# A Strassen-type output product of a SwiGLU layer: the second round of products accumulated on sums of the first, weight sums formed in place, and the GpSimd additions between the rounds taken out

## The chip, the cores and the metric

The kernel runs on one core of a Trainium2 chip. The metric is the device time of one execution in microseconds. A run gives a time of its own; a profiled execution gives a span (first to last instruction) and, beside it, that execution's time. All times of instructions below are microseconds from the start of the span.

## The reference, cut to what matters

The program is one decoder layer (sequence of 512, model width 1024): a token-mixing part with three gated branches, then a feed-forward part. Only the last product of the feed-forward part is touched here.

```python
x = x + merged @ w_o[l]
hf = rms_norm(x, ffn_norm_g[l]) @ w_ffn_in[l]
gt, up = jnp.split(hf, 2, axis=-1)
x = x + (jax.nn.silu(gt) * up) @ w_ffn_out[l]      # (512 x 2816) @ (2816 x 1024)
return x
```

All inputs and outputs are fp32. The kernel does each fp32 product as three TensorE products of split operands: a high part (fp32r, a ScalarE cast into a `wh` tile) and a low part (a VectorE difference into a `wl` tile); the function `mm3` issues hi x hi, hi x lo and lo x hi.

## The kernel before

The 2816 hidden columns are taken in two chunks (lines 890 to 902): 12 blocks of 128 first, then 10. For each chunk `ffn_in` computes the gated hidden activations and `quarters` (line 761) writes the seven left operands of a Strassen-type scheme for each pair of blocks; then `ffn_out` (line 806) multiplies them by `w_ffn_out` and adds the result to the residual stream `x1`. With `n` pairs (6, then 5), the scheme cuts the weight of a pair into four 128x512 quarters b11, b12, b21, b22 and needs seven products 1 to 7. Each product has two row blocks of 128 (`i` = 0, 1), so it fills two PSUM banks of 128x512 and takes 2 x 3 = 6 matmuls a pair. PSUM has eight banks here: four with the tag `mm`, three with `z`, one with `o`.

Seven products of two banks would need 14 banks, so the work is done in two rounds. The first round (lines 827 to 842) runs products 1, 7 and 6 over all pairs. The second (lines 854 to 872) runs products 2, 3, 4 and 5 over all pairs, product 2 on the banks `p1` that product 1 has left there. Between the rounds (lines 845 to 852) ScalarE copies p1 to SBUF (s1), VectorE forms s2 = p6 + s1 and s3 = p7 + s2 (temporaries of tag `t`, six buffers), and GpSimd adds s2 and s3 to three of the four quadrants of `x1` (tile `v` in the profile). Then product 3 takes a `z` and the `o` bank, product 4 two `mm` banks, product 5 two `z` banks. In the last pair the second round's products run in reverse (5, 4, 3, 2), and line 876 adds the banks to `x1`. In the second chunk (`last`) the final additions go to `t` temporaries which ScalarE's queue writes to `out` (line 878).

A pair's weights come by one DMA on SyncE's queue into a `raw` tile (three buffers). Its operands are made by `wsplit`: a ScalarE cast (line 81) and a VectorE difference (line 82), into `wh` and `wl` tiles of three buffers each, two per pair: in the second round first the one for products 2 and 3 (b21, b22 as loaded), then the one for products 4 and 5 (weight sums t1 and t4, lines 861 to 865, made in a `tt` tile of two buffers, with one `t` temporary for a partial sum). A `wh` buffer comes free when the matmuls that read it are done.

TensorE's instructions stand in the order of the source; on the other engines a scheduler orders them by priority (`tc.high_priority` moves loads and weight sums ahead), and each engine runs its own list strictly in order.

Of the kernel before, what the change touches and what calls it, by code (L numbers as in the profile page):

```python
# [11 lines left out]
ALU = mybir.AluOpType  # L12
# [23 lines left out]
def hybrid_layer(ctx, tc, x, mix_norm_g, w_in, q_norm_g, k_norm_g, w_attn_out, conf_dw_w,  # L36
# [5 lines left out]
    nc = tc.nc  # L42
    x, w_in, w_o = x[0], w_in[0], w_o[0]
# [16 lines left out]
    def alloc(tag, shape=(P, S), dt=F32):  # L60
        count[0] += 1
        where = ps if tag in ("mm", "z", "o") else odd if tag in ("c", "cf") else sb
        return where.tile(list(shape), dt, tag=tag, name=f"{tag}_{count[0]}", bufs=BUFS[tag])

    def psum(tag="mm"):
        return alloc(tag)

    def tmp(dt=F32, shape=(P, S)):
        return alloc("t", shape, dt)
# [22 lines left out]
    def mm3(o, a, b, start, stop):  # L92
        mm(o, a[0], b[0], start, False)
        mm(o, a[0], b[1], False, False)
        mm(o, a[1], b[0], False, stop)
# [45 lines left out]
    def wsplit(src):  # L141
        nsplit[0] += 1
        kt, n = src.shape[1], src.shape[2]
        with tc.high_priority(), ExitStack() as behind:
            for ins in queued_after.get(nsplit[0], ()):
                behind.enter_context(tc.issue_after(ins))
            hi, lo = alloc("wh", (P, kt, n), F32R), alloc("wl", (P, kt, n), F32R)
            split_to(hi, lo, src, sub=nc.gpsimd.tensor_sub if nsplit[0] in POOLW else None)
        return hi, lo
# [125 lines left out]
    with tc.high_priority(offset=1000000):  # L275
        for t in range(NT):
# [10 lines left out]
            last = nc.scalar.activation(y, y, AF.Exp, scale=-0.5)  # L287
# [518 lines left out]
    def ffn_out(j0, h, last):  # L806
        n = len(h)
        rows_of = lambda j, k: w_ffn_out[(j0 + 2 * j + k) * P:(j0 + 2 * j + k + 1) * P]

        def products(j, p, w, banks, start, stop):  # L810
            for i in range(2):
                a = [t[:, i * P:(i + 1) * P] for t in h[j][p]]
                mm3(banks[i], a, w, start and j == 0, stop and j == n - 1)

        def parts(src):
            hi, lo = wsplit(src)
            return [(hi[:, i], lo[:, i]) for i in range(src.shape[1])]

        def sums(fn):
            with tc.high_priority():  # L820
                t = alloc("tt", (P, 2, S))
                fn(t[:, 0], t[:, 1])
            return t


        p1, p6, p7 = [[psum(tag) for _ in range(2)] for tag in ("mm", "mm", "z")]
        for j in range(n):
            with tc.high_priority():
                w = alloc("raw", (P, 3, S))
                nc.sync.dma_start(w[:, 0:2], rows_of(j, 0).rearrange("p (n f) -> p n f", n=2))  # L830
                nc.sync.dma_start(w[:, 2], rows_of(j, 1)[:, S:])
            b11, b12, b22 = [w[:, i] for i in range(3)]

            def t32(t3, t2):
                nc.vector.tensor_sub(t3, b22, b12)
                nc.vector.tensor_add(t2, t3, b11)

            one, = parts(w[:, 0:1])
            t3, t2 = parts(sums(t32))
            products(j, 1, one, p1, True, True)  # L840
            products(j, 7, t3, p7, True, True)
            products(j, 6, t2, p6, True, True)

        x = lambda i, c: x1[c][:, i, :]
        for i in range(2):
            s1, s2, s3 = tmp(), tmp(), tmp()
            nc.scalar.copy(s1, p1[i])
            nc.vector.tensor_add(s2, p6[i], s1)  # L848
            nc.vector.tensor_add(s3, p7[i], s2)
            nc.gpsimd.tensor_add(x(i, 1), x(i, 1), s2)  # L850
            nc.gpsimd.tensor_add(x(i + 2, 0), x(i + 2, 0), s3)
            nc.gpsimd.tensor_add(x(i + 2, 1), x(i + 2, 1), s3)
        p3, p4, p5 = [[psum(tag) for tag in tags] for tags in (("z", "o"), ("mm", "mm"), ("z", "z"))]
        for j in range(n):
            with tc.high_priority():
                w = alloc("raw", (P, 2, 2, S))
                nc.sync.dma_start(w, w_ffn_out[(j0 + 2 * j) * P:(j0 + 2 * j + 2) * P].rearrange(
                    "(k p) (n f) -> p k n f", p=P, n=2))
            (b11, b12), (b21, b22) = [[w[:, k, i] for i in range(2)] for k in range(2)]

            def t14(t1, t4):
                v = tmp()
                nc.vector.tensor_sub(t1, b12, b11)
                nc.vector.tensor_sub(v, b22, b21)  # L864
                nc.vector.tensor_sub(t4, v, t1)  # L865

            two, three = parts(w[:, 1])
            t1, t4 = parts(sums(t14))
            order = [(2, two, p1, False), (3, three, p3, True), (4, t4, p4, True),
                     (5, t1, p5, True)]  # L870
            for p, part, banks, start in order if j < n - 1 else order[::-1]:
                products(j, p, part, banks, start, True)

        def add(i, c, p, final, op=nc.vector.tensor_add):
            y = tmp() if last and final else x(i, c)
            op(y, x(i, c), p)  # L876
            if last and final:
                nc.scalar.dma_start(out[i * P:(i + 1) * P, c * S:(c + 1) * S], y)

        for i in range(2):  # L880
            add(i, 1, p5[i], False)
            add(i + 2, 1, p5[i], True)
        for i in range(2):
            add(i + 2, 0, p4[i], True, nc.vector.tensor_sub)
        for i in range(2):
            add(i, 1, p3[i], True)
        for i in range(2):
            add(i, 0, p1[i], True)

    j0 = 0  # L890
    for c, n in enumerate((12, 10)):
        h = []
        queue.extend(ffn_in(j0, n, h, {k: list(v) for k, v in SPACE.items()}))
        if c == 0:
            tick(4)
            for square in [turn(f) for f in range(4, KT)]:
                square()
            tick(1)
            second_norm()
        drain()  # L900
        ffn_out(j0, h, c == 1)
        j0 += n
# [31 lines left out]
```

## Time and profile before

| | |
|---|---|
| median of 3 runs | 858.46 us (857.78 to 859.46) |
| the profiled execution's own time | 858.28 us |
| its span | 856.2 us |
| TensorE (PE) busy | 826.7 us, 97% of the span |
| VectorE (DVE) busy | 612.6 us, 72% |
| ScalarE (ACT) busy | 393.0 us, 46% |
| GpSimd (POOL) busy | 53.5 us, 6% |
| mean granted TensorE clock | 0.986 |
| first change of rounds (6 pairs) | about 636 to 655 us |
| second change of rounds (5 pairs) | about 810 to 829 us |

A row of the timeline has the start, the length, the engine, the line, the operation, output<-inputs by tile tag, the shape, the count of instructions merged into the row, and in square brackets the idle time of the engine ahead of it with what ended it. A row of the chain has start, length, engine, output tag, line and count. The view of stretches gives busy time of each engine (and number of instructions) between two points, with the granted TensorE clock (PEclk, 1.00 is full).

### The profile page before, as it was taken

How to read it: one execution, taken by the hardware profiler on the slowest of the kernel's cores; microseconds unless marked ns; L12 is line 12 of the kernel's file. 1: busy time of each engine (PE TensorE's matmuls, PEld its weight loads, DVE VectorE, ACT ScalarE, POOL GpSimd, SP SyncE). 2: the span in 40 equal slices, each digit the busy share in tenths (PEclk: the TensorE clock that was granted, in tenths of full speed). 3: DMA queues.
4: the chain of work that ended last, by engine and by line, in shares of the span. 5: the costliest groups of instructions: out<-in, count | busy, mean ns of one | idle time of the engine just before them, and what ended most of it. 6: DMA issues, size and time to landing. Idle time of an engine off the chain costs nothing.

```text
span 856.2 us, 9698 instructions
## 1 busy us (share of the span) xinstructions
PE 826.7 (97%) x3727; PEld 685.4 (80%) x3727; DVE 612.6 (72%) x878; ACT 393.0 (46%) x577; POOL 53.5 (6%) x72
## 2 busy tenths in 40 slices
PE   6999999999999999999999999999996999999967
PEld 6888887888888888888888888888875788888846
DVE  6598699896999998865443565556689645566895
ACT  6346689876663222753333453333332323333521
POOL 3100011101000000000001200000012000000040
PEclk9999999999999999999999999999997999999979
DMA  7333023131113323222452133322354422323532
GB/s 247 103 98 124 25 68 129 50 99 50 50 50 106 107 84 129 80 87 98 151 194 99 50 98 99 99 96 77 111 185 147 148 99 98 99 87 111 184 99 98
DMA packets 71274, 90.11 MB, mean 105 GB/s; under 512 B 1920, under 2 KB 56380, under 8 KB 71228
## 3 DMA queue, kind: packets, MB, share of 16 engines
q1 hardware_dynamic: 70060, 87.39, 31.0%
q10 hardware_dynamic: 1168, 2.10, 0.6%
q8 instruction: 29, 0.48, 0.2%
q14 instruction: 17, 0.14, 0.1%
HBM read 87.39 MB, written 2.10 MB: 105 GB/s over the span
## 4 chain that ended last, share of the span: by engine, by line
PE 91%; DVE 6%; issue 1%; ACT 1%; DMA 1%; SPq 0%; DVEq 0%
PE mm L90 76%; PE z L90 11%; PE o L90 3%; DVE t L864 1%; DVE wl L82 1%; DVE tt L865 1%; DMA m<-in_x_dram 1%; DVE cf L502 0%; DVE t L876 0%; PE mm L705 0%; DVE t L848 0%; DVE v L876 0%; ACT wh L81 0%; DVE t L283 0%; DVE t L82 0%
## 5 line engine op out<-in xcount | busy, mean ns | idle before, releaser
L90 PE MATMUL mm<-u,wh 128*128 128x512 f32 x1536 | 474.8, 390 | 1.0 <-DVE v L876 1.0
L90 PEld LDWEIGHTS mm<-u,wh 128*128 128x128 f32 x1536 | 287.3, 188 | 60.6 <-issue 1.4
L90 PE MATMUL mm<-u,wl 128*128 128x512 f32 x768 | 299.2, 390 | 0.0
L81 ACT CAST wh<-raw 128x1024 fp32r<-128x1024 f32 (+1 forms) x154 | 147.0, 955 | 286.8 <-PE mm L90 230.8
L82 DVE TENSOR_TENSOR wl<-raw,wh 128x1024 fp32r<-128x1024 f32 (+1 forms) x152 | 168.6, 1109 | 66.3 <-ACT wh L81 65.8
L90 PEld LDWEIGHTS mm<-u,wl 128*128 128x128 f32 x768 | 144.2, 188 | 30.2
L502 DVE SCALAR_TENSOR_TENSOR cf<-cf,cols_w,cf 128x512 f32<-128x512 f32 x120 | 89.9, 750 | 3.7 <-ACT cf L500 1.2
L793 DVE TENSOR_TENSOR t<-mm,cf 128x512 f32<-128x512 f32 x22 | 15.2, 691 | 59.6 <-PE mm L90 59.6
L90 PE MATMUL mm<-wh,m 128*128 128x512 f32 x104 | 37.4, 412 | 13.5 <-ACT wh L81 13.5
L81 ACT CAST wh<-tt 128x1024 fp32r<-128x1024 f32 x22 | 23.1, 1052 | 44.4 <-DVE tt L865 20.9
L90 PE MATMUL mm<-m,wh 128*128 128x512 f32 x128 | 39.4, 389 | 0.0
L90 PEld LDWEIGHTS mm<-wh,m 128*128 128x128 f32 x104 | 20.9, 201 | 18.7 <-ACT wh L81 14.4
L82 DVE TENSOR_TENSOR wl<-tt,wh 128x1024 fp32r<-128x1024 f32 x22 | 26.9, 1222 | 10.0 <-ACT wh L81 9.9
L791 DVE TENSOR_TENSOR t<-mm,cf 128x512 f32<-128x512 f32 x22 | 15.1, 688 | 25.9 <-PE mm L90 25.8
L90 PE MATMUL z<-wh,m 128*128 128x512 f32 x84 | 31.5, 415 | 0.0
L90 PEld LDWEIGHTS mm<-m,wh 128*128 128x128 f32 x128 | 24.0, 188 | 4.9
L78 ACT ACTIVATE s<-s 128x384 f32<-128x384 f32 (+1 forms) x48 | 26.9, 561 | 1.2
L717 POOL TENSOR_TENSOR cf<-cf,t 128x512 f32<-128x512 f32 x7 | 9.9, 1417 | 255.3 <-ACT t L715 255.0
L850 POOL TENSOR_TENSOR v<-v,t 128x512 f32<-128x512 f32 x4 | 6.0, 1502 | 310.6 <-DVE t L848 310.6
L90 PE MATMUL mm<-m,wl 128*128 128x512 f32 x64 | 24.9, 389 | 0.0
L90 PE MATMUL mm<-wh,b 128*128 128x512 f32 x72 | 23.9, 389 | 0.0
L90 PE MATMUL mm<-wl,m 128*128 128x512 f32 x52 | 21.5, 414 | 1.8 <-DVE wl L82 1.8
(254 smaller groups left out, 1087.8 us busy)
## 6 DMA issues: line engine op xcount, KB each, us to landing
raw<-in_w_in_dram SPq DMA_DIRECT2D x23, 1024.0 KB
raw<-in_w_ffn_in_dram SPq DMA_DIRECT2D x22, 1024.0 KB
raw<-in_w_ffn_out_dram SPq DMA_DIRECT2D x11, 1024.0 KB
raw<-in_w_ffn_out_dram SPq DMA_DIRECT2D x11, 512.0 KB
raw<-in_w_in_dram SPq DMA_DIRECT2D x10, 512.0 KB
raw<-in_w_o_dram SPq DMA_DIRECT2D x4, 1024.0 KB
raw<-in_w_ffn_out_dram SPq DMA_DIRECT2D x11, 256.0 KB
m<-in_x_dram SPq DMA_DIRECT2D x8, 256.0 KB
```

The costliest lines, as they stand in the source:

```text
L78: table(nc.scalar.activation(o, i, f, **kw))
L81: (copy or nc.scalar.copy)(hi, src)
L82: (sub or nc.vector.tensor_sub)(lo, src, hi.bitcast(F32))
L90: nc.tensor.matmul(o, lhsT, rhs, start=start, stop=stop, skip_group_check=True)
L502: nc.vector.scalar_tensor_tensor(y, pad[:, n:n + S], w(n), y, ALU.mult, ALU.add)
L717: nc.gpsimd.tensor_add(sumsq, sumsq, s)
L791: nc.vector.tensor_mul(g, pg[0], rstd[0])
L793: nc.vector.tensor_mul(u, pu, rstd[0])
L850: nc.gpsimd.tensor_add(x(i, 1), x(i, 1), s2)
L864: nc.vector.tensor_sub(v, b22, b21)
L865: nc.vector.tensor_sub(t4, v, t1)
```

## The change

Between the rounds ScalarE copies p1 to s1 as before, VectorE forms s2 = p6 + s1, and ScalarE now copies s2 into the PSUM banks of product 5 (a `z` and the `o` bank), on which product 5 then accumulates. VectorE adds p7 to one quadrant of `x1` and overwrites p7 in its banks by -p7 - s2 (line 855); product 4 accumulates on these. s3 and all GpSimd additions between the rounds are gone. Product 3 takes the banks of p6. The weight sums need no temporary: the second difference is written to its place and then reduced there. The second round's order is 2, 3, 5, 4, and 3, 5, 4, 2 in the last pair; the first round's is 1, 6, 7. At the end of the second chunk the banks of p5 are added twice: once by VectorE, and once through a ScalarE copy and a GpSimd addition (lines 885 to 889). The diff:

```diff
--- before.py
+++ after.py
@@ -838,19 +838,22 @@
             one, = parts(w[:, 0:1])
             t3, t2 = parts(sums(t32))
             products(j, 1, one, p1, True, True)
+            products(j, 6, t2, p6, True, True)
             products(j, 7, t3, p7, True, True)
-            products(j, 6, t2, p6, True, True)
+
 
         x = lambda i, c: x1[c][:, i, :]
+        p5 = [psum(tag) for tag in ("z", "o")]
+        s2 = [tmp(), tmp()]
         for i in range(2):
-            s1, s2, s3 = tmp(), tmp(), tmp()
+            s1 = tmp()
             nc.scalar.copy(s1, p1[i])
-            nc.vector.tensor_add(s2, p6[i], s1)
-            nc.vector.tensor_add(s3, p7[i], s2)
-            nc.gpsimd.tensor_add(x(i, 1), x(i, 1), s2)
-            nc.gpsimd.tensor_add(x(i + 2, 0), x(i + 2, 0), s3)
-            nc.gpsimd.tensor_add(x(i + 2, 1), x(i + 2, 1), s3)
-        p3, p4, p5 = [[psum(tag) for tag in tags] for tags in (("z", "o"), ("mm", "mm"), ("z", "z"))]
+            nc.vector.tensor_add(s2[i], p6[i], s1)
+            nc.scalar.copy(p5[i], s2[i])
+        for i in range(2):
+            nc.vector.tensor_add(x(i + 2, 1), p7[i], x(i + 2, 1))
+            nc.vector.scalar_tensor_tensor(p7[i], p7[i], -1.0, s2[i], ALU.mult, ALU.subtract)
+        p3, p4 = [psum("mm") for _ in range(2)], p7
         for j in range(n):
             with tc.high_priority():
                 w = alloc("raw", (P, 2, 2, S))
@@ -859,16 +862,16 @@
             (b11, b12), (b21, b22) = [[w[:, k, i] for i in range(2)] for k in range(2)]
 
             def t14(t1, t4):
-                v = tmp()
                 nc.vector.tensor_sub(t1, b12, b11)
-                nc.vector.tensor_sub(v, b22, b21)
-                nc.vector.tensor_sub(t4, v, t1)
+                nc.vector.tensor_sub(t4, b22, b21)
+                nc.vector.tensor_sub(t4, t4, t1)
 
             two, three = parts(w[:, 1])
             t1, t4 = parts(sums(t14))
-            order = [(2, two, p1, False), (3, three, p3, True), (4, t4, p4, True),
-                     (5, t1, p5, True)]
-            for p, part, banks, start in order if j < n - 1 else order[::-1]:
+            order = [(2, two, p1, False), (3, three, p3, True), (5, t1, p5, False),
+                     (4, t4, p4, False)]
+            for k in range(4) if j < n - 1 else (1, 2, 3, 0):
+                p, part, banks, start = order[k]
                 products(j, p, part, banks, start, True)
 
         def add(i, c, p, final, op=nc.vector.tensor_add):
@@ -878,12 +881,17 @@
                 nc.scalar.dma_start(out[i * P:(i + 1) * P, c * S:(c + 1) * S], y)
 
         for i in range(2):
-            add(i, 1, p5[i], False)
-            add(i + 2, 1, p5[i], True)
+            add(i, 1, p3[i], False)
+        for i in range(2):
+            add(i, 1, p5[i], True)
+            if last:
+                s1 = tmp()
+                nc.scalar.copy(s1, p5[i])
+                add(i + 2, 1, s1, True, nc.gpsimd.tensor_add)
+            else:
+                add(i + 2, 1, p5[i], True)
         for i in range(2):
             add(i + 2, 0, p4[i], True, nc.vector.tensor_sub)
-        for i in range(2):
-            add(i, 1, p3[i], True)
         for i in range(2):
             add(i, 0, p1[i], True)
 
```

The scheduler's lists move with it. **VectorE at the first change of rounds.** In these rows `raw`, `wh`, `wl` and `tt` numbers that grow are those of later pairs: in the first list raw_5212, 5251 and 5290 are the second round's first three pairs; mm_4992 and 4993 are p6, z_4994 and 4995 are p7. Before:

```order
L863 TENSOR_TENSOR tt_5257<-raw_5251 128x512
L82 TENSOR_TENSOR wl_5215<-raw_5212,wh_5214 128x1024
L848 TENSOR_TENSOR t_5189<-mm_4992,t_5188 128x512
L849 TENSOR_TENSOR t_5190<-z_4994,t_5189 128x512
L848 TENSOR_TENSOR t_5198<-mm_4993,t_5197 128x512
L849 TENSOR_TENSOR t_5199<-z_4995,t_5198 128x512
L864 TENSOR_TENSOR t_5219<-raw_5212 128x512
L864 TENSOR_TENSOR t_5258<-raw_5251 128x512
L864 TENSOR_TENSOR t_5297<-raw_5290 128x512
L865 TENSOR_TENSOR tt_5218<-t_5219,tt_5218 128x512
L865 TENSOR_TENSOR tt_5257<-t_5258,tt_5257 128x512
L82 TENSOR_TENSOR wl_5224<-tt_5218,wh_5223 128x1024
```

And now, where raw_5244 and 5282 are the second and third pairs (the first pair's and the second's sums, tt_5212 and tt_5250, stand above these rows):

```order
L82 TENSOR_TENSOR wl_5217<-tt_5212,wh_5216 128x1024
L851 TENSOR_TENSOR t_5190<-mm_4992,t_5192 128x512
L865 TENSOR_TENSOR tt_5288<-raw_5282 128x512
L866 TENSOR_TENSOR tt_5288<-raw_5282 128x512
L82 TENSOR_TENSOR wl_5247<-raw_5244,wh_5246 128x1024
L867 TENSOR_TENSOR tt_5288<-tt_5288 128x512
L851 TENSOR_TENSOR t_5191<-mm_4993,t_5196 128x512
L854 TENSOR_TENSOR v_3713<-z_4994,v_3713 128x512
L855 SCALAR_TENSOR_TENSOR z_4994<-z_4994,t_5190 128x512
L854 TENSOR_TENSOR v_3713<-z_4995,v_3713 128x512
L82 TENSOR_TENSOR wl_5255<-tt_5250,wh_5254 128x1024
L855 SCALAR_TENSOR_TENSOR z_4995<-z_4995,t_5191 128x512
```

The first pair's weight sums and their low part moved from behind the sums of the first round to ahead of them; work for the second and third pairs (wl_5247, wl_5255, tt_5288) now stands among the steps that free the banks.

**ScalarE at the same place, now.** mm_4990 and 4991 are p1, z_5188 and o_5189 the banks of product 5:

```order
L81 CAST wh_5208<-raw_5206 128x1024
L850 COPY t_5192<-mm_4990 128x512
L81 CAST wh_5216<-tt_5212 128x1024
L850 COPY t_5196<-mm_4991 128x512
L81 CAST wh_5246<-raw_5244 128x1024
L852 COPY z_5188<-t_5190 128x512
L852 COPY o_5189<-t_5191 128x512
L81 CAST wh_5254<-tt_5250 128x1024
```

The two copies into PSUM stand behind the second pair's first cast, which takes the buffer wh_5166 of the last pair of the first round.

**ScalarE's queue at the end of the program.** Before it held eight writes in the order of VectorE's additions. Now, with t_6585, 6593, 6601, 6604, 6607 and 6610 from VectorE, t_6590 and 6598 from GpSimd:

```order
L881 DMA out_dram<-t_6585 128x512
L889 COPY t_6588<-z_6375 128x512
L881 DMA out_dram<-t_6590 128x512
L881 DMA out_dram<-t_6593 128x512
L889 COPY t_6596<-o_6376 128x512
L881 DMA out_dram<-t_6598 128x512
L881 DMA out_dram<-t_6601 128x512
L881 DMA out_dram<-t_6604 128x512
L881 DMA out_dram<-t_6607 128x512
L881 DMA out_dram<-t_6610 128x512
```

Two copies and two writes of GpSimd's results came in ahead of the last four writes.

## The prediction, made before the changed kernel was run

> **What bounds the kernel now.** I read the page first, for its engine rows and the chain that ended last.
>
> ```profile
> span 856.2 us, 9698 instructions
> PE 826.7 (97%) x3727; PEld 685.4 (80%) x3727; DVE 612.6 (72%) x878; ACT 393.0 (46%) x577; POOL 53.5 (6%) x72
> PE 91%; DVE 6%; issue 1%; ACT 1%; DMA 1%; SPq 0%; DVEq 0%
> ```
>
> TensorE is the bound: only where it waits, or runs slowly, can this change win anything, since it leaves the count of matmuls as it is. The profiled execution took 858.28 us, 2.1 more than its span and 0.2 under the median, so terms taken from it carry over.
>
> Second, the chain in order of time at the first change of rounds, to see who holds TensorE:
>
> ```profile
> 638.55 0.70 DVE t L848
> 640.60 0.69 DVE t L849
> 641.29 4.46 DVE t L864 x3
> 645.76 3.34 DVE tt L865 x2
> 649.10 1.15 DVE wl L82
> 650.29 2.50 PE mm L90 x5
> ```
>
> The chain leaves TensorE for 11.7 us and goes through VectorE: four sums of the first round, then five weight-sum instructions of three pairs, then the low part of t4 and t1. Third, the timeline of TensorE at both changes of rounds:
>
> ```profile
> 638.74 0.39 PE L90 MATMUL mm<-wh,l 128*128 128x512 f32 x1
> 640.55 0.39 PE L90 MATMUL z<-wl,m 128*128 128x512 f32 x1
> 641.46 0.39 PE L90 MATMUL o<-wh,m 128*128 128x512 f32 x1
> 648.61 0.79 PE L90 MATMUL mm<-wh,m 128*128 128x512 f32 x1 [6.77 <-ACT wh L81]
> 650.29 0.80 PE L90 MATMUL mm<-wl,m 128*128 128x512 f32 x1 [0.89 <-DVE wl L82]
> 655.09 0.40 PE L90 MATMUL mm<-wh,m 128*128 128x512 f32 x1
> 815.24 0.39 PE L90 MATMUL o<-wh,m 128*128 128x512 f32 x1
> 822.40 0.80 PE L90 MATMUL mm<-wh,m 128*128 128x512 f32 x1 [6.76 <-ACT wh L81]
> 828.93 0.47 PE L90 MATMUL mm<-wh,m 128*128 128x512 f32 x1
> ```
>
> Matmuls start 0.226 us apart (640.55 to 641.46 is four of them). From 641.46 to 655.09 there are 13 starts: the one at 641.46 and the twelve of products 4 and 5. They should take 2.94 us and took 13.63: **10.7 us lost**. At the second change, 815.24 to 828.93, it is 13.69 - 2.94, 10.75. The waits are 7.7 us of each; the rest is the clock, as the view of stretches shows:
>
> ```profile
> core 0: us, PE busy (x) PEld busy (x) DVE busy (x) ACT busy (x) POOL busy (x), PEclk, DMA share, GB/s
> 641.34:644.75 3.41, 0.50 (x3) 0.08 (x1) 3.41 (x3) 0.00 (x0) 3.41 (x3) 1.00 0.34 65
> 648.17:651.58 3.41, 2.08 (x4) 1.38 (x5) 3.41 (x4) 2.29 (x3) 0.38 (x1) 0.50 0.00 0
> 655.00:658.41 3.41, 3.41 (x16) 2.79 (x16) 2.04 (x3) 1.37 (x2) 0.00 (x0) 1.00 0.18 73
> 682.30:685.71 3.41, 2.43 (x11) 1.92 (x11) 3.41 (x6) 1.05 (x1) 0.00 (x0) 1.00 0.02 5
> 849.55:852.97 3.42, 1.43 (x7) 0.85 (x5) 2.78 (x5) 0.00 (x0) 0.00 (x0) 1.00 1.03 397
> 852.97:856.19 3.22, 0.00 (x0) 0.00 (x0) 0.00 (x0) 0.00 (x0) 0.00 (x0) 0.50 0.40 151
> ```
>
> PEclk changes only at the ends of these 3.41 us stretches. After one with 0.50 us of matmuls it was halved, after one with 1.43 too (the program's end), after one with 2.43 it was not.
>
> **What goes: the wait for the weight sums.** The rows that price VectorE, ScalarE and GpSimd here:
>
> ```profile
> 639.32 1.30 POOL L850 TENSOR_TENSOR v<-v,t 128x512 f32<-128x512 f32 x1 [146.03 <-DVE t L848]
> 633.45 1.23 DVE L82 TENSOR_TENSOR wl<-tt,wh 128x1024 fp32r<-128x1024 f32 x1 [1.14 <-ACT wh L81]
> 634.71 0.69 DVE L863 TENSOR_TENSOR tt<-raw 128x512 f32<-128x512 f32 x1
> L847 ACT COPY t<-mm x4: 576/585/592, 636.0 to 810.3; 128x512 f32<-128x512 f32 x4
> L81 ACT CAST wh<-tt x4: 1050/1054/1056, 658.1 to 674.4; 128x1024 fp32r<-128x1024 f32 x4
> L710 DVE SCALAR_TENSOR_TENSOR u<-mm,cols,u x7: 744/747/751, 461.5 to 486.6; 128x512 fp32r<-128x512 f32 x7
> ```
>
> A weight sum takes 0.69 us alone (634.71), but the three of line 864 took 4.46 and the two of line 865 3.34, 1.5 to 1.7 each, while GpSimd's six additions ran (from 639.32 on). With those gone the slowing goes. And the first two pairs' sums now stand ahead of s2, in VectorE time that lay idle. So the old wait goes entirely; the question is what is late next.
>
> **What is late next.** I follow the new lists with these lengths (starts of independent 512-wide steps 0.6 us apart, as 640.60 to 641.21 was for lines 849 and 864; a low part 1.14). VectorE ends the last low part of the first round at 634.7 as before, makes the second pair's three sums until 636.9, the low part for products 2 and 3 until 638.0, the one for 5 and 4 until 639.2, and s2 of row block 0 until 639.8. Then come two sums of the third pair (641.1) and a low part of the second pair, whose cast had to wait for the last first-round matmuls (638.74 + 0.39) and ended at 640.3; it is done at 642.2, the third sum at 642.9, s2 of block 1 at 643.5. TensorE meanwhile goes from the first round to product 2 at 638.97 (until 640.3) and product 3 block 0 (until 641.0). Product 3 block 1 needs p6's second bank, read by s2 of block 1: it **waits 641.0 to 643.5, 2.4 us**. Product 5 follows without a wait: its seeds, two ScalarE copies of 0.585, are there at 640.8 and 644.1. Product 4 block 0 is ready at 644.8. Block 1 of it stands behind the second pair's other low part, whose cast takes the buffer of products 2 and 3 and so waits for them (644.3): cast until 645.5, low part until 646.7, line 855 with 0.75 (line 710's length) until 647.4. TensorE is there at 646.2: **waits 1.2 us**. Then the second pair's operands are all ready, and each pair costs VectorE 3 x 0.69 + 2 x 1.14 = 4.4 us against 24 x 0.226 = 5.4 on TensorE, so no further wait. Sum: 3.6 us lost in place of 10.7. At the second change of rounds ScalarE's list has the copy of p1 block 1 late (behind the cast that waits for the first round's end), so product 2 waits for it, but the end is set by the same s2 and line 855: 3.7.
>
> No row shows ScalarE or VectorE writing PSUM. I take the lengths of reading it (0.585, 0.75). From below 0 for the seeds, which are ready 4 us ahead or follow a wait anyway; from above 1.23, the longest VectorE row here: 0.5 us more at line 855 per change.
>
> A wait of 2.4 us can leave one stretch with only 1.0 us of matmuls, less than the 1.43 that halved the clock, if it falls into one stretch; the stretches do not keep step with the program, so in part of the runs it is split. While the clock is half, VectorE catches up and the 1.2 us wait shrinks. I take 0.5 us per change for it (0 to 2.4): **4.1 lost, 6.6 gained, twice: -13.2**. The Trainium skill (TensorE: Matmul & The Clock Gate, Why this matters for your kernels) says that only idle gaps above about 3 us bring the clock down; by that the 0.5 goes and the time would be 1.0 us lower. The stretch with 1.43 us speaks for a stricter gate than that.
>
> **Between the chunks.**
>
> ```profile
> 682.10 0.39 PE L90 MATMUL mm<-wh,l 128*128 128x512 f32 x1
> 683.46 0.70 PE L90 MATMUL mm<-u,wh 128*128 128x512 f32 x2 [0.98 <-DVE v L876]
> ```
>
> The next chunk waits for an `mm` bank of product 4, whose addition stands late on VectorE. Now product 3 holds `mm` banks, is first in the last pair, and its addition is first: 683.46 - 682.10 - 0.23 = **-1.1** (0 to -1.1).
>
> **The end.**
>
> ```profile
> 848.06 0.68 DVE L876 TENSOR_TENSOR t<-v,z 128x512 f32<-128x512 f32 x1
> 850.59 0.39 PE L90 MATMUL mm<-wh,b 128*128 128x512 f32 x1
> 851.05 1.28 DVE L876 TENSOR_TENSOR t<-v,mm 128x512 f32<-128x512 f32 x2
> 852.36 0.34 ACTq L878 DMA_DIRECT2D out_dram<-t  x1
> L876 DVEq EVENT_SEMAPHORE  x4: 21/21/49, 848.3 to 850.8; - x4
> ```
>
> Before, the last matmul ended at E = 850.98 and the last write was issued at E + 1.4. Now ScalarE's strict list alternates. Product 5 block 0 ends at E - 3.4, VectorE's sum at E - 2.6, its write is issued until E - 2.2, the copy ends at E - 1.6, GpSimd's addition (1.30, beside VectorE work on PSUM as at 639.32) at E - 0.25; only then its write, block 1's write (until E + 0.5), the second copy (E + 1.1), GpSimd again (E + 2.4), and its write and four more, 0.34 each: the last is issued at E + 3.8. VectorE's last additions wait too, since six `t` buffers now carry ten tiles: the one of p1 block 0 for the write of GpSimd's first result (issued at E - 0.2, landed 2.1 later: the write of the sum of 848.06 had landed by 850.8), that of block 1 for GpSimd's second addition; done at E + 3.2, in time for ScalarE. So the end moves 2.4; five writes close together may take a little more: **+2.6** (1.5 to 3.5).
>
> Sum: 858.3 - 13.2 - 1.1 + 2.6 = **846.6 us**.
>
> **The rivals.** *The clock falls at both changes of rounds.* Then two stretches run at half rate, each worth up to 1.7 us, less what the waits overlap: 6.0 lost per change in place of 4.1, 846.6 + 3.8 = 850.4. For it: 1.43 us of matmuls in a stretch did not hold the clock. Against: the stretch with 2.43 held. The Trainium skill (TensorE: Matmul & The Clock Gate, A second HAM failure mode: psum-queue depth-cycling) describes just such short waits between groups bringing the clock down and up. 18%.
>
> *The waits vanish*, because TensorE's group boundaries and VectorE's steps fit better than my hand count: 10.7 gained twice, 858.3 - 21.4 - 1.1 + 2.6 = 838.4. Against: s2 of block 1 stands behind a cast that cannot start before the first round ends. 5%.
>
> *The old wait merely moves* (the change doesn't do what it says): the steps that seed banks stand on VectorE with 6 or 7 us of other work between them, and if each takes as long as beside GpSimd (1.5 us), the wait is some 6 us again with the clock down: 10 lost per change, 858.3 - 1.4 - 1.1 + 2.6 = 858.4. Against: the slow rows lie only beside GpSimd's. 4%.
>
> *Slower: the third pair's load holds VectorE.* Two sums of the third pair now stand between s2 of block 0 and of block 1, so its DMA, issued at about 632.8, must have landed by 639.7.
>
> ```profile
> 628.73 23.04 SPq L857 DMA_DIRECT2D raw<-in_w_ffn_out_dram  x4
> ```
>
> The second pair's load was issued at 628.73 and read at 634.71: 6.0 us at most, so 638.8, 0.9 us in time. Each us beyond costs one per change. It turns the result from a landing 8 us late on (14 us from issue), with the clock down as well: about 861. 3%.
>
> **How the numbers follow.** The forecast has 70%: 846.6, own range 843.5 to 849.5 from the ends of the end term, of the clock and of line 855. With the clock rival nearly all lies between 843.0 and 851.5. 0.2% (1.7 us) is about what a measurement here can tell from no change. The moved wait's 4% I split 1 faster, 2 same, 1 slower. Faster: 0.70 + 0.18 + 0.05 + 0.01 = 0.94; same 0.02; slower 0.03 + 0.01 = 0.04.
>
> **What would show it.** Right: no TensorE wait at line 90 above 3 us at either change of rounds; two short ones, released by VectorE (lines 851, 855) or ScalarE (850); line 865 to 867 at 0.69; no wait ahead of the second chunk's first matmul; a last write issued about 3.8 us after the last matmul's end, behind GpSimd. Wrong: waits near 7 us, PEclk 0.50 over three stretches, or a VectorE wait for a load.

## The result and the profile after

The changed kernel takes **846.9 us** (median of 4 runs, 845.98 to 848.2) against 858.9 for the kernel before (4 runs, 857.78 to 859.46): ratio 0.9863, 95% interval 0.9846 to 0.988. The forecast was 846.6, with a range of 843.0 to 851.5. The profiled execution took 846.77 us. Its page opens so:

```profile
span 845.0 us, 9697 instructions
PE 822.5 (97%) x3727; PEld 682.4 (81%) x3727; DVE 603.8 (71%) x880; ACT 396.3 (47%) x583; POOL 37.6 (4%) x62
```

The count of matmuls is the old one, and TensorE is still busy for 97% of a shorter span. What was removed is waiting. The timeline of TensorE at both changes of rounds:

```profile
641.67 0.39 PE L90 MATMUL mm<-wh,m 128*128 128x512 f32 x1
644.09 0.50 PE L90 MATMUL mm<-wh,m 128*128 128x512 f32 x1 [2.03 <-DVE t L851]
648.12 0.50 PE L90 MATMUL z<-wh,m 128*128 128x512 f32 x1 [1.01 <-DVE z L855]
648.92 0.40 PE L90 MATMUL mm<-wh,m 128*128 128x512 f32 x1
...
805.78 0.39 PE L90 MATMUL mm<-wh,m 128*128 128x512 f32 x1
807.63 0.50 PE L90 MATMUL mm<-wh,m 128*128 128x512 f32 x1 [1.46 <-ACT t L850]
809.93 0.50 PE L90 MATMUL mm<-wh,m 128*128 128x512 f32 x1 [0.64 <-DVE t L851]
813.96 0.50 PE L90 MATMUL z<-wh,m 128*128 128x512 f32 x1 [0.99 <-DVE z L855]
```

The waits of 6.8 us for a cast are gone; five short ones stand in their place, released by the steps that the forecast named. From 641.67 to 648.92 there are 16 starts, which at 0.2265 us each should take 3.6; they took 7.25. I do this sum for every kernel below in one way: over all starts from 632 to 665 us and from 796 to 829, what lies between two successive starts beyond 0.2265 us is counted as lost. Before: 10.8 and 10.8. After: **3.7 and 4.0**.

VectorE's list shows why the two waits have these places:

```profile
639.81 0.69 DVE L851 TENSOR_TENSOR t<-mm,t 128x512 f32<-128x512 f32 x1
640.41 0.68 DVE L865 TENSOR_TENSOR tt<-raw 128x512 f32<-128x512 f32 x1
...
642.75 0.69 DVE L867 TENSOR_TENSOR tt<-tt 128x512 f32<-128x512 f32 x1
643.35 0.69 DVE L851 TENSOR_TENSOR t<-mm,t 128x512 f32<-128x512 f32 x1
...
644.55 0.69 DVE L855 SCALAR_TENSOR_TENSOR z<-z,t 128x512 f32<-128x512 f32 x1
...
646.23 1.23 DVE L82 TENSOR_TENSOR wl<-tt,wh 128x1024 fp32r<-128x1024 f32 x1 [0.40 <-ACT wh L81]
647.37 0.69 DVE L855 SCALAR_TENSOR_TENSOR z<-z,t 128x512 f32<-128x512 f32 x1
```

Between the two sums of line 851 stand four instructions of later pairs, 2.9 us; TensorE waits 2.03 of them. The second line 855 stands behind a low part that itself waits for a cast. The weight sums (lines 865 to 867) take 0.69 each, where they took 1.5 to 1.7 before.

Ahead of the second chunk's first matmul there is no gap any more:

```profile
675.90 0.39 PE L90 MATMUL mm<-wh,l 128*128 128x512 f32 x1
676.13 0.62 PE L90 MATMUL mm<-u,wh 128*128 128x512 f32 x2
```

The end has grown. TensorE's last matmul, then ScalarE's queue and GpSimd:

```profile
836.31 0.39 PE L90 MATMUL mm<-wh,b 128*128 128x512 f32 x1
...
837.33 0.58 ACT L889 COPY t<-o 128x512 f32<-128x512 f32 x1 [2.26 <-DVE t L879]
838.04 1.26 POOL L879 TENSOR_TENSOR t<-v,t 128x512 f32<-128x512 f32 x1 [1.61 <-issue]
839.34 2.35 ACTq L881 DMA_DIRECT2D out_dram<-t  x5
```

The last matmul ends at E = 836.70 and the span 8.3 us later; before, it was 850.98 and 5.2. So the end costs **3.1 us**. The account against the kernel before: 21.5 - 7.7 = 13.8 us won at the changes of rounds, 1.1 at the chunk boundary, 3.1 lost at the end: 11.8 us, and the medians differ by 12.0. The two profiled executions differ by 11.5 (858.28 and 846.77). The one after is already 0.9 us behind the one before at 629 us, ahead of the changed lines, and got so within its first 15 us; in the other profiles below that start lies between 0.1 us earlier and 1.6 us later than in the kernel before. So an agreement of totals to a few tenths of a us says little.

### The profile page after: what moved, and what is told of

It is laid out like the page before. It is cut to its first block, busy times and chain, and to the rows that moved or that the text cites. A ratio compares the mean times of both kernels' runs of the same rounds, so it can differ in the third digit from the quotient of the medians.

```text
span 845.0 us, 9697 instructions
## 1 busy us (share of the span) xinstructions
PE 822.5 (97%) x3727; PEld 682.4 (81%) x3727; DVE 603.8 (71%) x880; ACT 396.3 (47%) x583; POOL 37.6 (4%) x62
## 5 line engine op out<-in xcount | busy, mean ns | idle before, releaser
L90 PE MATMUL mm<-wh,m 128*128 128x512 f32 x104 | 35.0, 392 | 4.1 <-DVE t L851 2.7
L448 DVE SCALAR_TENSOR_TENSOR s<-z,s 128x384 f32<-128x384 f32 (+1 forms) x24 | 14.4, 598 | 11.6 <-ACT s L78 10.4
L78 ACT ACTIVATE t<-t 128x512 f32<-128x512 f32 x31 | 19.6, 631 | 3.7 <-DVE t L791 3.7
L558 DVE TENSOR_TENSOR t<-mm,t 128x512 f32<-128x512 f32 x16 | 10.9, 689 | 14.0 <-PE mm L90 14.0
```

The lines of the kernel that those rows point to most:

```text
L78: table(nc.scalar.activation(o, i, f, **kw))
L90: nc.tensor.matmul(o, lhsT, rhs, start=start, stop=stop, skip_group_check=True)
L448: marks.append(nc.vector.scalar_tensor_tensor(t, z, 0.0, t, ALU.max, ALU.add))
L558: nc.vector.tensor_mul(s[0], y, s[0])
```

## The experiments

The change does three things at once at a change of rounds: it makes the weight sums in place, it takes GpSimd's additions away, and it puts sums into banks (with the order of the products that goes with them). Theory A of the first three runs is that the order was the old wait (the temporary held the sums behind the boundary); theory B is that GpSimd's slowing of VectorE was.

| kernel | median us | ratio to before (95%) | lost at the changes of rounds, us |
|---|---|---|---|
| before | 858.4 to 859.0 | | 10.8, 10.8 |
| after | 846.92 | 0.9863 (0.9846 to 0.988) | 3.7, 4.0 |
| sums in place only | 845.83 | 0.9851 (0.9837 to 0.9864) | 4.2, 3.9 |
| no GpSimd between rounds only | 853.26 | 0.9937 (0.9925 to 0.9949) | 7.6, 7.5 |
| after, temporary back | 856.69 | 0.9977 (0.9968 to 0.9986) | 9.9, 9.4 |
| after, banks first | 840.53 | 0.9789 (0.9775 to 0.9803) | 0.9, 0.7 |
| after, VectorE end | 844.01 | 0.9829 (0.9816 to 0.9842) | 3.7, 4.0 |
| after, writes on two queues | 845.49 | 0.9847 (0.9834 to 0.986) | 3.7, 4.1 |
| banks first, VectorE end | **837.58** | 0.9757 (0.9744 to 0.9769) | 0.9, 0.7 |
| later pairs behind, VectorE end | 838.03 | 0.9759 (0.9747 to 0.9772) | 0.1, 1.8 |
| before, in place, sums first | 843.00 | 0.9816 (0.9803 to 0.9829) | 2.9, 3.2 |
| the same without GpSimd | 839.46 | 0.9775 (0.9762 to 0.9789) | 1.3, 1.3 |

The last column is read from one profiled execution of each kernel, the medians are not. With GpSimd's additions alone taken away that execution was the fastest of five (851.81), with the temporary back the slowest of ten (857.94).

### Sums in place only

```diff
--- before
             def t14(t1, t4):
-                v = tmp()
                 nc.vector.tensor_sub(t1, b12, b11)
-                nc.vector.tensor_sub(v, b22, b21)
-                nc.vector.tensor_sub(t4, v, t1)
+                nc.vector.tensor_sub(t4, b22, b21)
+                nc.vector.tensor_sub(t4, t4, t1)
```

> The kernel before with one part of the change alone: the third weight sum is made in place (no temporary from the pool that the round's sums and the outputs share); GpSimd's additions between the rounds, the banks and the orders stay as before. Theory A (the temporaries held the second round's weight sums behind the round boundary; most of the wait was order, not slow rows): the sums of the first two pairs move ahead of the boundary, the loss at each change of rounds falls from 10.7 us to between 2.9 and 4.5, and the time to 843 to 846.5 (no longer end than before, no gain between the chunks). Rival B (GpSimd's six additions made VectorE's rows slow, 1.5 to 1.7 us in place of 0.69, and these slow rows were the wait): the slow rows stay, the loss stays near 9 or 10 each, the time is 855 or more.

845.83 us: theory A, at the upper half of its range. These three lines alone bring as much time as the whole change: 8.1 us stay lost at the changes of rounds against 7.7, with the old wait at the chunk boundary and the old, shorter end. The timeline of VectorE and, below it, of GpSimd in this kernel:

```profile
635.87 0.69 DVE L862 TENSOR_TENSOR tt<-raw 128x512 f32<-128x512 f32 x1
...
640.08 0.68 DVE L848 TENSOR_TENSOR t<-mm,t 128x512 f32<-128x512 f32 x1
...
649.46 1.77 DVE L863 TENSOR_TENSOR tt<-raw 128x512 f32<-128x512 f32 x1
```

```profile
648.95 1.74 POOL L850 TENSOR_TENSOR v<-v,t 128x512 f32<-128x512 f32 x1
650.65 1.74 POOL L851 TENSOR_TENSOR v<-v,t 128x512 f32<-128x512 f32 x1
```

The second pair's sums (from 635.87) now stand ahead of the round's own sums (640.08). The slow rows are still there, 1.77 us beside GpSimd, but all except one (line 863 at 641.28, 1.76 us) come once TensorE has operands in hand. What they still cost stands in the view of TensorE's waits (us in total, times, longest), 2.8 us over both changes:

```profile
PE mm L90 <- DVE wl L82: 2.8, 2, 1.6
```

### No GpSimd between the rounds, and nothing else

```diff
--- before
-            nc.gpsimd.tensor_add(x(i, 1), x(i, 1), s2)
-            nc.gpsimd.tensor_add(x(i + 2, 0), x(i + 2, 0), s3)
-            nc.gpsimd.tensor_add(x(i + 2, 1), x(i + 2, 1), s3)
+            nc.vector.tensor_add(x(i, 1), x(i, 1), s2)
+            nc.vector.tensor_add(x(i + 2, 0), x(i + 2, 0), s3)
+            nc.vector.tensor_add(x(i + 2, 1), x(i + 2, 1), s3)
```

> The kernel before with another part alone: the six additions between the rounds are made by VectorE in place of GpSimd; temporaries, banks and orders stay as before. Theory A (order): the weight sums still stand behind the boundary and now also behind six more additions of about 0.69 us, but each takes 0.69; about 7 us lost at each change of rounds in place of 10.7, time about 851.5. Rival B (contention is all of it): with rows of 0.69 the wait is gone but for some 3 us each, time about 845.

853.26 us: nearer to A, 1.8 us slower than it. VectorE's rows and TensorE's:

```profile
642.88 0.69 DVE L849 TENSOR_TENSOR t<-z,t 128x512 f32<-128x512 f32 x1
643.49 1.88 DVE L864 TENSOR_TENSOR t<-raw 128x512 f32<-128x512 f32 x3
```

```profile
647.16 0.80 PE L90 MATMUL mm<-wh,m 128*128 128x512 f32 x1 [4.85 <-ACT wh L81]
```

The three sums of line 864 take 1.88 us in place of 4.46. So B is a true mechanism. But they still stand behind line 849, TensorE still waits 4.85 us, and the first matmul after it (0.80) shows the clock at half: 7.5 us stay lost.

### The temporary back

```diff
--- after
             def t14(t1, t4):
+                v = tmp()
                 nc.vector.tensor_sub(t1, b12, b11)
-                nc.vector.tensor_sub(t4, b22, b21)
-                nc.vector.tensor_sub(t4, t4, t1)
+                nc.vector.tensor_sub(v, b22, b21)
+                nc.vector.tensor_sub(t4, v, t1)
```

> The kernel after with one part of the change undone: the third weight sum has its temporary again. No GpSimd between the rounds, banks and orders of the change as after. Theory A (order): the sums of later pairs stand between and behind the steps that seed the banks, and line 855 far behind them; at least 8 us lost at each change in place of 3.6 to 4.0, time 854 to 857. Rival B (it was GpSimd's contention): rows stay at 0.69, little is lost, about 847.

856.69 us (10 runs): A. Without the edit in place the rest of the change is worth 1.9 us, after paying for its longer end (8.1 us from the last matmul to the end of the span, 5.2 before). VectorE and TensorE:

```profile
639.32 1.89 DVE L867 TENSOR_TENSOR t<-raw 128x512 f32<-128x512 f32 x3
...
649.42 0.69 DVE L855 SCALAR_TENSOR_TENSOR z<-z,t 128x512 f32<-128x512 f32 x1
```

```profile
650.16 0.80 PE L90 MATMUL z<-wh,m 128*128 128x512 f32 x1 [4.45 <-DVE z L855]
```

No row is slow, GpSimd does nothing between the rounds, and TensorE waits 4.45 us and comes out of the wait at half the clock (0.80). It waits for line 855, which starts at 649.42 here and at 644.55 in the kernel after, because ten weight sums and three low parts of later work stand between (from 639.32 on). Three runs together settle it: the order is the larger cause, GpSimd's slowing the smaller.

### Banks first

The two loops of lines 848 to 855 are put under a higher rank, else unchanged:

```diff
--- after
-        for i in range(2):
-            s1 = tmp()
-            nc.scalar.copy(s1, p1[i])
-            nc.vector.tensor_add(s2[i], p6[i], s1)
...
+        with tc.high_priority(offset=1000000):
+            for i in range(2):
+                s1 = tmp()
+                nc.scalar.copy(s1, p1[i])
+                nc.vector.tensor_add(s2[i], p6[i], s1)
...
```

> The kernel after, with the steps that give the banks of the first round free (ScalarE's copies of lines 850 and 852, VectorE's of lines 851, 854 and 855) ranked ahead of every weight sum, so that on VectorE they stand directly behind the second pair's low part for products 2 and 3 and ahead of its other low part and of the third pair's sums. Theory (the two waits that are left are the places of s2 of block 1 and of line 855 in VectorE's list): the waits for lines 851 and 855 (2.0 and 1.0 us at the first change) go, a wait of about 1.0 for the second pair's other low part is left, 2.6 us are won at each change: 846.9 - 5.2 = 841.7, say 841.3 to 842.5. Rival (TensorE's pace after the change of rounds is set by how fast VectorE turns out operands, in whatever order): the waits only move, 846 to 848.

840.53 us, 0.8 better than the theory's range. This kernel has one line more, so lines 851, 854 and 855 are 852, 855 and 856 here. In VectorE's list they now stand directly behind each other:

```profile
637.66 1.28 DVE L852 TENSOR_TENSOR t<-mm,t 128x512 f32<-128x512 f32 x2
...
639.45 0.69 DVE L856 SCALAR_TENSOR_TENSOR z<-z,t 128x512 f32<-128x512 f32 x1
...
640.65 0.69 DVE L856 SCALAR_TENSOR_TENSOR z<-z,t 128x512 f32<-128x512 f32 x1
```

One wait per change is left:

```profile
642.51 0.50 PE L90 MATMUL z<-wl,m 128*128 128x512 f32 x1 [0.57 <-DVE wl L82]
...
804.99 0.50 PE L90 MATMUL z<-wl,m 128*128 128x512 f32 x1 [0.34 <-DVE wl L82]
```

The lost time falls from 7.7 to 1.6 us: 6.1 won, and 846.92 - 6.1 = 840.8. I had put the wait for the low part at 1.0; it is 0.57 and 0.34. So the two waits were places in a list, not a lack of VectorE time.

### The end on VectorE, and the writes on two queues

```diff
--- after (first kernel)
             add(i, 1, p5[i], True)
-            if last:
-                s1 = tmp()
-                nc.scalar.copy(s1, p5[i])
-                add(i + 2, 1, s1, True, nc.gpsimd.tensor_add)
-            else:
-                add(i + 2, 1, p5[i], True)
+            add(i + 2, 1, p5[i], True)
--- after (second kernel)
-                nc.scalar.dma_start(out[i * P:(i + 1) * P, c * S:(c + 1) * S], y)
+                (nc.scalar if c else nc.sync).dma_start(out[i * P:(i + 1) * P, c * S:(c + 1) * S], y)
```

> The kernel after, but at the program's end the last two additions of product 5 (to the two lower quadrants of column 1) are made by VectorE straight from the bank, without ScalarE's copy and without GpSimd. In the kernel after, the last write is issued 4.5 us after the last matmul's end and the span ends 8.3 us after it; before it was 1.4 and 5.2. Theory: the end is the chain of ScalarE's copy, GpSimd's addition (1.26 to 1.29 us) and the writes queued behind it in ScalarE's strict list; without it the last write is issued about 1.4 us after the last matmul and the time falls by 3.1 us, from 846.9 to about 843.8. Rival: the end is bound by the traffic of the last writes themselves, whoever makes the sums; the time stays within 0.7 us of 846.9.

> The kernel after, with the writes of column 0 (the last four of the eight) issued by SyncE's queue in place of ScalarE's, where they stand behind GpSimd's. Theory (five writes queued back to back in one list cost 0.47 us each where paced ones cost 0.34, and the first of them waits for GpSimd's second result): the last write is then issued when VectorE's last sum is ready, about 3.4 us after the last matmul's end in place of 4.5; about 1.2 us won, 845.7. Rival (the writes' traffic, or the landing of each, sets the end): within 0.5 us of 846.9.

844.01 and 845.49 us: the theory both times. The last matmul and ScalarE's queue in the first kernel, then the last matmul and SyncE's queue in the second:

```profile
835.61 0.39 PE L90 MATMUL mm<-wh,b 128*128 128x512 f32 x1
...
833.35 4.52 ACTq L881 DMA_DIRECT2D out_dram<-t  x8
```

```profile
835.81 0.39 PE L90 MATMUL mm<-wh,b 128*128 128x512 f32 x1
...
836.68 3.21 SPq L881 DMA_DIRECT2D out_dram<-t  x4
```

With VectorE alone the last issue is over at 837.87, 1.9 us after the last matmul's end there (835.61 + 0.39). With two queues the last issue is over at 839.89, 3.7 us after it (835.81 + 0.39), where the kernel after needs 5.0 (841.69). So GpSimd's chain was 2.9 of the 3.1 us by the medians (2.8 by the time from the last matmul to the end of the span, 5.5 in place of 8.3). The writes standing in line behind its second result were about 1 of these: 1.4 by the medians, 1.3 by the last issue, 0.9 by the end of the span. VectorE, which the change relieved by two additions there, had the time for them.

### Banks first with the end on VectorE, and later pairs behind

The first joins the two edits above. The second leaves the ranks alone and only holds back two groups at the change of rounds (besides the end on VectorE):

```diff
--- after
-            nc.vector.scalar_tensor_tensor(p7[i], p7[i], -1.0, s2[i], ALU.mult, ALU.subtract)
+            freed = nc.vector.scalar_tensor_tensor(p7[i], p7[i], -1.0, s2[i], ALU.mult, ALU.subtract)
...
-            two, three = parts(w[:, 1])
-            t1, t4 = parts(sums(t14))
+            with ExitStack() as behind:
+                if j == 1:
+                    behind.enter_context(tc.issue_after(freed.ins))
+                two, three = parts(w[:, 1])
+            with ExitStack() as behind:
+                if j == 2:
+                    behind.enter_context(tc.issue_after(freed.ins))
+                sums14 = sums(t14)
+            t1, t4 = parts(sums14)
```

> The last order (banks first) together with the end on VectorE, which alone took 2.9 us off the kernel after. If the two gains add: the time of the kernel with the banks first less 2.9, about 838.6. Rival: the end's gain depends on how the cores of work lie there; less than 1.5 us.

> The end on VectorE, and only two groups of instructions held back at the change of rounds: the second pair's part for products 2 and 3 (its first cast and low part) and the third pair's sums are issued behind the last line 855; the second pair's... other work stays where the order has it. Theory (as for banks first): at the first change of rounds nothing to 0.5 us is lost in place of 3.6; at the second s2 of block 1 comes to stand behind lines 854 and 855 of block 0, so 1 to 2 us are left there; 844.0 - 3.3 - 2.5 = about 838, 837 to 840. Rival (VectorE's pace): 843 or more.

837.58 and 838.03 us: the gains add, and both beat both kernels. Banks first loses 0.9 and 0.7 us at the changes. Later pairs behind loses 0.1 at the first; at the second one wait of 1.46 us is left, for ScalarE's copy of line 850 as in the kernel after (807.63). The size is the expected one, the cause is not: s2 of block 1 does stand behind lines 854 and 855 of block 0 (at 804.48), but what TensorE waits for is the copy.

### What the sums in the banks are worth: the kernel before with the round's sums first

Both kernels start from the sums in place; the second has `vector` where the first has `gpsimd`.

```diff
--- sums in place only
-        for i in range(2):
-            s1, s2, s3 = tmp(), tmp(), tmp()
...
+        s2, s3 = [tmp(), tmp()], [tmp(), tmp()]
+        with tc.high_priority(offset=1000000):
+            for i in range(2):
+                s1 = tmp()
+                nc.scalar.copy(s1, p1[i])
+                nc.vector.tensor_add(s2[i], p6[i], s1)
+                nc.vector.tensor_add(s3[i], p7[i], s2[i])
+        for i in range(2):
+            nc.gpsimd.tensor_add(x(i, 1), x(i, 1), s2[i])
+            nc.gpsimd.tensor_add(x(i + 2, 0), x(i + 2, 0), s3[i])
+            nc.gpsimd.tensor_add(x(i + 2, 1), x(i + 2, 1), s3[i])
```

> The kernel before with the weight sums in place (845.8 by the run of that alone) and with its round sums (the copies, s2, s3) ranked ahead of every weight sum; the six additions stay on GpSimd. In the run with the sums in place TensorE still waited 1.1 and 0.4 us for s2 of block 1, 0.9 at each change for the copy of product 1's first bank, and 1.2 and 1.6 for low parts of weights, which VectorE made late because its rows beside GpSimd's additions took 1.7 us in place of 0.69. Theory: only the first wait goes, 845.8 - 1.5 = 844.3, and GpSimd's slowing still costs about 2.8. Rival (order alone sets it): the slowed rows find cover, 841.5 or less.

> The same with the six additions on VectorE, behind the round sums and spread between the weight sums by the scheduler: no sum is made in a bank, and GpSimd does nothing between the rounds. Theory (of the change's two parts behind the order, it is GpSimd's slowing that costs, and the banks that hold sums are worth nothing by themselves): its waits for low parts go, some 0.9 for a copy at each change is left, 844.3 - 2.8 = 841.5, 840.5 to 842.5. Rival (VectorE has no room for six more additions of 0.69 at each change; that is what the sums in the banks save): 844 to 848.

843.00 and 839.46 us. The first lies between theory and rival, a little nearer to the theory. The second is 1.0 us below the range of its theory, on the side away from the rival. The wait for s2 is gone, the waits beside GpSimd are not: TensorE's waits with GpSimd, and below without.

```profile
PE mm L90 <- DVE wl L82: 3.0, 2, 1.7
PE mm L90 <- ACT t L849: 1.9, 2, 0.9
PE mm L90 <- DVE v L878: 1.0, 1, 1.0
```

```profile
PE mm L90 <- ACT t L849: 1.9, 2, 0.9
PE mm L90 <- DVE v L878: 1.0, 1, 1.0
```

Once the order is right, GpSimd's slowing is worth 3.5 us, and VectorE has room for six more additions per change. The best kernel with sums in the banks is 1.9 us faster than this one without them. Its waits differ by as much: here 0.97 at the chunk boundary and 1.9 for two copies, there 0.9 for low parts, so 2.0. TensorE waits for a copy at each change because the second copy of p1 stands behind a cast in ScalarE's list here (copy at 640.67, cast at 639.71); in the best kernel it stands ahead of it (638.99 and 641.17). I take this for a place that could be changed without the banks, but did not try it. If so, about 1 us, the chunk boundary, is left for the banks and the new orders of products; which of the two brings it was not tried either.

## Why the prediction was right

The time came out 0.3 us above the forecast, and the mechanism was the one that the sum describes: the old wait gone, two short ones in its place, a longer end. Two of its terms were off by about half a us each, in opposite directions.

- **"So the old wait goes entirely."** It does. But the prediction named GpSimd's slowing first and the sums' new place second. The runs turn this round: the place alone gives 12.7 us, GpSimd's removal alone 5.3, and the rest of the change without the place 1.9 net of the longer end. The first two do not add, as either edit shortens the same wait. So the forecast that the wait goes did not depend on the weight given to its two causes, and the right number says nothing about it.
- **The two short waits, 2.4 and 1.2.** Measured 2.03 and 1.01 at the first change, with the same releasers. Both waits were shorter than forecast, together by 0.6, and about 0.3 more is lost around each (behind the first, the next start comes 0.33 us later, 644.09 to 644.42, in place of 0.2265), which the forecast did not count. So 3.7 lost, forecast 3.6, is in part luck. At the second change 4.0, forecast 3.7, with ScalarE's late copy in the place foreseen (1.46).
- **Half a us per change for the clock.** Nothing: it held at full rate at both changes. So 4.1 per change was 0.25 too much on average, a gain of 13.8 where 13.2 was forecast. In the profiled execution the rival with the clock down did not occur. The stretches with the fewest matmuls, one at each change:

```profile
642.94:646.35 3.41, 2.26 (x10) 1.88 (x11) 3.01 (x6) 1.64 (x2) 0.00 (x0) 1.00 0.71 227
806.78:810.19 3.41, 1.92 (x7) 1.31 (x8) 3.41 (x6) 1.08 (x3) 0.00 (x0) 1.00 0.67 197
```

  The 1.0 us of matmuls that the prediction feared in one stretch did not come about: the wait of 2.03 us lay across two stretches, 1.92 us was the least, and neither stretch brought the clock down.
- **Line 855 and the copies into PSUM**, priced at 0.75 and 0.585 from rows that read it: 0.69 and 0.58 to 0.59. The upper bound of 1.23 was far off.
- **The chunk boundary, -1.1**: exactly so, 0.23 between the two starts.
- **The end, +2.6: the mis-sized term, 3.1.** The chain was right (copy, GpSimd, then a queue of writes); the step that failed is "its write and four more, 0.34 each". Five writes in a row took 2.35 us, 0.47 each, and the first of them began at E + 2.6 where 2.4 was forecast. The forecast had allowed 0.2 us for writes close together; with the late start the term is 0.5 short.
- **The third pair's load** was in time: the first sum of it (640.41) follows line 851 with no idle time.
- **The waits vanish** was given 5%. They can vanish, all but 1.6 us, by rank alone (banks first); in the order as built they do not.

The two errors, 0.6 at the changes and 0.5 at the end, had opposite signs. That is why the total was closer than its terms, and so close a total is luck.

## What to carry to other kernels

A temporary taken from a small pool is a place in an order: a sum that needs one cannot stand ahead of the work that holds the pool's buffers, and here writing it in place was worth more than taking GpSimd's slowing away (12.7 us against 5.3). Whether a larger pool would have done the same was not tried. At a boundary between phases, first rank the steps that free buffers for the bound engine ahead of everything that prepares later work; only then ask which engine should do them. Price a program's last engine-queue chain with the writes behind it: work moved there onto a slower engine has nothing behind it that could hide it (2.8 of the 3.1 us at the end here).

## What the runs showed of the hardware

- **VectorE and GpSimd share something, but not for every operand.** In the kernel with the round's sums first and GpSimd between the rounds, VectorE's rows and GpSimd's:

```profile
642.71 2.33 DVE L82 TENSOR_TENSOR wl<-raw,wh 128x1024 fp32r<-128x1024 f32 x1
644.96 0.68 DVE L851 TENSOR_TENSOR t<-z,t 128x512 f32<-128x512 f32 x1
645.57 1.18 DVE L866 TENSOR_TENSOR tt<-raw 128x512 f32<-128x512 f32 x1
```

```profile
642.67 1.29 POOL L854 TENSOR_TENSOR v<-v,t 128x512 f32<-128x512 f32 x1
643.92 2.28 POOL L855 TENSOR_TENSOR v<-v,t 128x512 f32<-128x512 f32 x1
```

 The low part with two SBUF inputs took 2.33 us in place of 1.22, while GpSimd's addition beside it kept 1.29; 1.1 us longer, about that addition's length. The sum with one input in PSUM kept its 0.68 in the middle of a GpSimd addition. The Trainium skill (SBUF — State Buffer, Who interferes with whom) says that the two engines share a port pair under an exclusive lock, that a VectorE instruction with two SBUF inputs contends with a GpSimd instruction that reads SBUF, and that one with at most one SBUF input (outside the 2-port modes) does not. These rows agree with both halves.

- **Whether the clock fell went by a stretch's matmul time, with the limit near half of it.** In the kernel with the temporary back:

```profile
643.24:646.65 3.41, 1.72 (x6) 0.86 (x5) 3.41 (x4) 1.61 (x2) 0.00 (x0) 1.00 0.53 147
646.65:650.07 3.42, 0.00 (x0) 0.00 (x0) 3.42 (x7) 0.00 (x0) 0.00 (x0) 0.50 0.71 287
```

 1.72 us of matmuls in a stretch (50%), and the clock was halved in the next, 0.9 us into a wait. In the kernel with two write queues a stretch with 1.70 was not followed by that (its clock stayed at full rate until 840.15, behind the last matmul):

```profile
806.01:809.43 3.42, 1.70 (x7) 1.09 (x7) 3.42 (x6) 1.09 (x4) 0.00 (x0) 1.00 0.61 211
```

 So these rows place the limit near half and no closer; 1.92 held above, and 1.43 fell in the kernel before. From 100 us on, every full-rate stretch in the twelve profiles that kept its clock had 1.70 us of matmuls or more, and every one that lost it 1.72 or less. The Trainium skill (TensorE: Matmul & The Clock Gate, Why this matters for your kernels) speaks of idle gaps above about 3 us. The clock of the kernel after agrees, with no gap above 2.03 up to its last matmul; the first of these stretches does not, since it has 1.7 us without matmuls in all and the clock fell at its end.

- **Issuing a write costs ScalarE's queue 0.34 us when writes come 0.6 us apart, and 0.47 when they come in a row** (2.35 for five, above). Why is open.
